# Upper and lower parts of stationary weights element by element in one tile, 128 bytes off a multiple of 256

## The chip, the cores and the metric

The kernel runs on one core of one Trainium2 chip. The metric is device time in microseconds of one execution. TensorE multiplies, ScalarE (ACT) and VectorE (DVE) move and convert tiles, GpSimd (POOL) helps with sums, SyncE (SP) issues the large DMAs.

## The reference

Two pre-norm residual layers over 512 tokens of width 1024, each a token mixer and a squared-ReLU MLP, all in float32:

```python
for i in range(DEPTH):                       # DEPTH = 2
    h = rmsnorm(x, norm_mix_g[i])
    if i % N_MIXERS == 0:
        h = chunked_spatial_gating(h, a_w_in, a_b_in, a_v_norm_g, a_w_s, a_b_s, a_w_out)
    else:
        h = retention(h, b_w_in, b_head_norm_g, b_w_out)
    x = x + h
    h = rmsnorm(x, norm_ffn_g[i])
    x = x + squared_relu_mlp(h, mlp_w1[i], mlp_w2[i])   # relu(h @ w1) ** 2 @ w2, width 4096
return rmsnorm(x, final_norm_g)
```

The gating mixer projects to two halves `u` and `v` of width 2048, mixes `v` over chunks of 128 tokens and multiplies. The retention mixer has four heads with queries and keys of 256, values of 512 and a gate `g`.

## The kernel before

Every large product is made of three matmuls on numbers of type fp32r, which TensorE reads at one pass. Both factors are split into an upper part (the value rounded to fp32r, names ending in H) and a lower part (what is left, names ending in L), and `mm3` adds upper by upper, upper by lower and lower by upper into one PSUM tile. In the profile these are lines 215, 216 and 217. In "out<-a,b" of a matmul, a is the moving operand (512 columns mostly) and b the stationary one (128 by 128, loaded by an LDWEIGHTS, shown as PEld, before its matmul).

The weights are 60 raw tiles of 1 MB, each brought by DMA into one of two buffers (`RAW_BUFS`) and cut into two pieces of 128 partitions by 1024 elements. There are three ways to cut:

- `pieces_f`: eight blocks of 128 by 128 along the contraction. The weights are stationary and the activations moving. It serves `up`, `dn` (the down projection of layer 0), `u`, `g`, `qk`.
- `pieces_o`: four blocks of 128 by 256, stationary too, for the mixers' output projections `o` and `ro`.
- `pieces_t`: two blocks of 128 by 512. The weights are moving, and slices of the activations are stationary. It serves `v`, `vv` and `dt` (the down projection of layer 1).

A piece takes 24 matmuls, with 8 to 16 more of another kind between pieces where attention, gating or transposes need them. The order of the work is written out by hand: `step` appends a function and its pieces to a list, and the last loop runs the list. In each step the function issues the matmuls, then `advance()` (the second halves of earlier evacuations), then `refill()`, then the evacuation of its own result.

`refill` prepares pieces ahead. `prep` takes the next piece of the order: it has the DMA of a coming raw tile issued on SP (`load_raws`), takes tiles (`prep_tiles`), has ScalarE round the raw piece into the upper part (the CAST of line 179), and has VectorE subtract that from the raw piece into the lower part (line 183). Upper parts are made three pieces ahead (`LOOK`) in four buffers, lower parts two ahead in three buffers. An engine works through its queue in order; semaphores hold it where a buffer is not free or an input is missing.

Where things lie: in each partition, `xT`, `hH`, `hL`, the raw tiles, the upper and lower weight tiles and the ten large buffers of the activations start on a multiple of 2048 bytes. The small constants do not: `onesr`, the all-ones stationary matrix of the norm's sums, starts at byte 17024, which is 128 more than a multiple of 256. Upper and lower weights are contiguous, 4096 bytes per partition each.

Of the kernel before, what the change touches and what calls it, by code (L numbers as in the profile page):

```python
# [11 lines left out]
F32R = mybir.dt.float32r  # L12
# [5 lines left out]
P = 128  # L18
# [14 lines left out]
class Raw:  # L33


    def __init__(self, src, parts=1):
        self.src, self.parts, self.tile, self.done = src, parts, None, 0


class Piece:  # L40


    def __init__(self, raw, view, shape):
        self.raw, self.view, self.shape = raw, view, shape
        self.hi = self.lo = None


def pieces_f(w, rows, cols):
# [9 lines left out]
def pieces_t(w, rows, cols, parts=1):  # L58

    out = []  # L60
    for r in range(rows[0], rows[1], 512):
        raw = Raw(w[r : r + 512, cols[0] : cols[1]].rearrange("(k p) n -> p k n", p=P), parts)
        for i in range(2):
            out.append(Piece(raw, (slice(None), slice(2 * i, 2 * i + 2), slice(None)), [P, 2, 512]))
    return out


# [11 lines left out]
def trunk(ctx, tc, x, norm_mix_g, norm_ffn_g, a_w_in, a_b_in, a_v_norm_g, a_w_s, a_b_s, a_w_out,  # L79
          b_w_in, b_head_norm_g, b_w_out, mlp_w1, mlp_w2, final_norm_g, trig, decay, out):  # L80
    nc = tc.nc
# [3 lines left out]
    wts = ctx.enter_context(tc.tile_pool(name="wts", bufs=3))  # L85
# [1 line left out]
    work = ctx.enter_context(tc.tile_pool(name="work", bufs=2))  # L87
    psum = ctx.enter_context(tc.tile_pool(name="psum", bufs=6, space=PSUM))

    RAW_BUFS, LOOK = 2, 3  # L90

    def big(shape, dt, name):
        return bigp.tile(shape, dt, tag="big", name=name)
# [16 lines left out]
    def f32(ap):  # L110
        return ap.bitcast(F32)
# [48 lines left out]
    def load_raws(upto):  # L160
        while pos["raw"] < min(upto, len(raws)):
            r = raws[pos["raw"]]
            while r.done < r.parts:
                load_part(r)
            pos["raw"] += 1

    def prep_tiles(i):
        p = order[i]
        p.hi = wts.tile(p.shape, F32R, tag="wH", name=f"wH{i}", bufs=4)
        p.lo = wts.tile(p.shape, F32R, tag="wL", name=f"wL{i}", bufs=3)  # L170

    def prep(upto, low=None):

        low = upto if low is None else low
        while pos["piece"] < min(upto, len(order)):
            p = order[pos["piece"]]
            load_raws(raws.index(p.raw) + RAW_BUFS)
            prep_tiles(pos["piece"])
            nc.scalar.copy(out=p.hi, in_=p.raw.tile[p.view])  # L179
            pos["piece"] += 1  # L180
        while pos["low"] < min(low, len(order)):
            p = order[pos["low"]]
            nc.vector.tensor_sub(out=p.lo, in0=p.raw.tile[p.view], in1=f32(p.hi))  # L183
            pos["low"] += 1

    def launch(g):
# [11 lines left out]

    def refill():
        n = pos["done"]  # L200
        prep(n + (LOOK if n >= 4 else 1), n + (LOOK - 1 if n >= 4 else 1))

    def step(fn, *ps):
        for p in ps:
# [107 lines left out]
    def feat(p, bufs, evac, name, behind=None):  # L312

        def run(p):
            ps = acc(name)
            mm_f(p, ps, *bufs(), range(8), 7)
            advance()
            refill()
            if behind:
                behind()  # L320
            launch(evac(ps))
        step(run, p)

    def feat_late(p, q, evacs, name):

        def run(p, q):
            pa, pb = acc(f"{name}a"), acc(f"{name}b")
            flush()
            for r, ps in ((p, pa), (q, pb)):
                mm_f(r, ps, hH, hL, range(7), 7)  # L330
            for r, ps in ((p, pa), (q, pb)):
                mm_f(r, ps, hH, hL, [7], 7)
            advance()
            refill()
            launch(evacs[0](pa))
            launch(evacs[1](pb))
        step(run, p, q)

    def tokens(plist, bufs, evac, name, behind=None, last=None):

        accs = {}
        behind = behind or {}

        def one(i):
            def run(p):
                if i == 0:
                    for n in range(NT):
                        accs[n] = acc(f"{name}_{n}")
                aH, aL = bufs()
                for n in range(NT):  # L350
                    s = slice(n * P, (n + 1) * P)
                    for k in range(2):
                        kk = 2 * i + k
                        mm3(accs[n], aH[kk][:, s], aL[kk][:, s], p.hi[:, k, :], p.lo[:, k, :], kk == 0, kk == 7)
                advance()
                refill()
                if i in behind:
                    behind[i]()
                if i == 3:
                    for n in range(NT):  # L360
                        launch(evac(n, accs[n]))
            return run

        for i, p in enumerate(plist[:2] if last else plist):
            step(one(i), p)
        if last:
            step(lambda *ps: last(bufs, accs, evac, *ps), *plist[2:])
# [161 lines left out]

    nrm = norm("mix0")  # L530
    vl = [pieces_t(win, (0, D), (GW + 512 * j, GW + 512 * (j + 1)), parts=4 if j == 0 else 1) for j in range(4)]
    accs0 = {}

    def two_chunks(i):

        prep(i + 2)
        for k in (2 * i + 2, 2 * i + 3):
            x_chunk(k)
        for k in (2 * i, 2 * i + 1):
            squares(k, MIX)  # L540

    def v0(i):
        def run(p):
            if i == 0:
                for n in range(NT):
                    accs0[n] = acc(f"v0_{n}")
            if i in (1, 2):
                two_chunks(i)
            for k in range(2):
                kk = 2 * i + k  # L550
                if i == 0 and k == 1:
                    two_chunks(0)
                if i == 3:
                    prep(5 + k)
                    if k == 0:
                        squares(6, MIX)
                        squares(7, MIX)
                    next(nrm)
                wh, wl = p.hi[:, k, :], p.lo[:, k, :]
                for j, (h, w) in enumerate(((hH, wh), (hH, wl), (hL, wh))):  # L560
                    for n in range(NT):
                        nc.tensor.matmul(accs0[n], lhsT=h[kk][:, n * P : (n + 1) * P], rhs=w, start=kk == 0 and j == 0, stop=kk == 7 and j == 2)
                if i == 2 and k == 0:
                    columns(rows, 16, 80)
            if i == 3:
                for n in range(NT):
                    launch(evac_v(0)(n, accs0[n]))
                next(nrm)
        return run
# [236 lines left out]
    def v_unit(h, behind=None):  # L806
        tokens(pieces_t(bw, (0, D), (VW + h * DV, VW + (h + 1) * DV)), hs, evac_vv(h), f"vv{h}", behind)
# [112 lines left out]
    def down_t(q):  # L920
        do(flush)
        for c in range(2):
            tokens(pieces_t(mlp_w2[1], (1024 * q, 1024 * (q + 1)), (512 * c, 512 * (c + 1))), acts(q), evac_last(q, c), f"dt{q}{c}",
                   last=ends if q == 3 and c == 1 else None)
# [32 lines left out]
    for _ in range(5):  # L957
        nc.tensor.matmul(warm[:, 0:P], lhsT=ident, rhs=ident, start=True, stop=True)
    columns(rows2, 0, 16)
    prep_tiles(0)  # L960
    for k in range(2):
        p = order[0]
# [56 lines left out]
```

## Time and profile before

| | |
|---|---|
| median of 3 runs | 1406.9 us (1406.83 to 1407.25) |
| profiled execution | 1407.72 us, span of its instructions 1406.0 us |
| TensorE busy with matmuls | 1390.5 us, 6290 matmuls |
| TensorE busy with weight loads | 1155.4 us, 6290 loads |
| VectorE / ScalarE / GpSimd busy | 793.0 / 507.2 / 127.7 us |
| casts of weights (ScalarE) | 239, mean 1045 ns |
| subtractions of weights (VectorE) | 239, mean 1282 ns |
| DMA | 135.23 MB, mean 96 GB/s |

The durations of matmuls overlap, since a matmul starts before the one ahead has drained. What a matmul costs is the distance between its start and the next one's. Weight loads run beside matmuls. The granted TensorE clock is 0.998 of full speed on average.

### The profile page before, as it was taken

How to read it: one execution, taken by the hardware profiler on the slowest of the kernel's cores; microseconds unless marked ns; L12 is line 12 of the kernel's file. 1: busy time of each engine (PE TensorE's matmuls, PEld its weight loads, DVE VectorE, ACT ScalarE, POOL GpSimd, SP SyncE). 2: the span in 40 equal slices, each digit the busy share in tenths (PEclk: the TensorE clock that was granted, in tenths of full speed). 3: DMA queues.
4: the chain of work that ended last, by engine and by line, in shares of the span. 5: the costliest groups of instructions: out<-in, count | busy, mean ns of one | idle time of the engine just before them, and what ended most of it. 6: DMA issues, size and time to landing. Idle time of an engine off the chain costs nothing.

```text
span 1406.0 us, 15372 instructions
## 1 busy us (share of the span) xinstructions
PE 1390.5 (99%) x6290; PEld 1155.4 (82%) x6290; DVE 793.0 (56%) x1102; ACT 507.2 (36%) x721; POOL 127.7 (9%) x98
## 2 busy tenths in 40 slices
PE   8999999999999999999999999999999999999997
PEld 7888888888888888888888888888888888888885
DVE  6757765775444445476647574564685443434335
ACT  4656633334413223123334323333334422313222
POOL 3010111220000000011111100110130000000002
PEclk9999999999999999999999999999999999999999
DMA  6332222232223322423222131132122332232221
GB/s 225 109 116 90 72 90 88 81 120 90 90 90 104 106 90 90 148 89 108 90 78 72 60 120 60 62 118 90 61 90 91 120 104 90 93 117 91 90 90 60
DMA packets 106101, 135.23 MB, mean 96 GB/s; under 512 B 2400, under 2 KB 79792, under 8 KB 105776
## 3 DMA queue, kind: packets, MB, share of 16 engines
q1 hardware_dynamic: 106000, 134.26, 29.4%
q8 instruction: 49, 0.80, 0.2%
q14 instruction: 20, 0.16, 0.0%
q10 hardware_dynamic: 32, 0.01, 0.0%
HBM read 132.16 MB, written 2.10 MB: 95 GB/s over the span
## 4 chain that ended last, share of the span: by engine, by line
PE 96%; DVE 3%; POOL 0%; ACT 0%; DMA 0%; issue 0%; SPq 0%; ACTq 0%; DVEq 0%
PE up L217 8%; PE up L216 8%; PE up L215 8%; PE dn L217 4%; PE dn L216 4%; PE dn L215 4%; PE dt L216 4%; PE dt L217 4%; PE dt L215 4%; PE g L215 2%; PE qk L215 2%; PE vv L216 2%; PE g L216 2%; PE vv L215 2%; PE g L217 2%; PE vv L217 2%
## 5 line engine op out<-in xcount | busy, mean ns | idle before, releaser
L183 DVE TENSOR_TENSOR wL<-raw,wH 128x1024 fp32r<-128x1024 f32 x239 | 305.9, 1282 | 112.8 <-PE dt L216 65.5
L179 ACT CAST wH<-raw 128x1024 fp32r<-128x1024 f32 x239 | 249.7, 1045 | 264.7 <-PE dt L217 114.9
L215 PE MATMUL up<-hH,wH 128*128 128x512 f32 x480 | 187.2, 390 | 0.0
L217 PE MATMUL up<-hH,wL 128*128 128x512 f32 x480 | 186.8, 389 | 0.0
L216 PE MATMUL up<-hL,wH 128*128 128x512 f32 x480 | 186.8, 389 | 0.0
L631 DVE TENSOR_TENSOR aH<-r 128x512 fp32r<-128x512 f32 x64 | 45.0, 703 | 159.5 <-ACT r L629 159.4
L216 PEld LDWEIGHTS up<-hL,wH 128*128 128x128 f32 x480 | 90.1, 188 | 18.7
L215 PEld LDWEIGHTS up<-hH,wH 128*128 128x128 f32 x480 | 90.1, 188 | 18.7
L217 PEld LDWEIGHTS up<-hH,wL 128*128 128x128 f32 x480 | 90.1, 188 | 18.7
L215 PE MATMUL dn<-aH,wH 128*128 128x512 f32 x256 | 99.6, 389 | 0.0
L216 PE MATMUL dn<-aL,wH 128*128 128x512 f32 x256 | 99.6, 389 | 0.0
L217 PE MATMUL dn<-aH,wL 128*128 128x512 f32 x256 | 99.6, 389 | 0.0
L215 PE MATMUL dt<-wH,aH 128*128 128x512 f32 x256 | 99.6, 389 | 0.0
L216 PE MATMUL dt<-wL,aH 128*128 128x512 f32 x256 | 99.6, 389 | 0.0
L217 PE MATMUL dt<-wH,aL 128*128 128x512 f32 x256 | 99.6, 389 | 0.0
L629 ACT ACTIVATE r<-up 128x512 f32<-128x512 f32 x60 | 35.9, 598 | 166.7 <-PE up L217 166.7
L239 POOL TENSOR_TENSOR ssq<-ssq,sq 128x512 f32<-128x512 f32 x28 | 43.0, 1537 | 401.6 <-ACT sq L238 401.3
L501 DVE TENSOR_TENSOR xs<-dn,wide 128x512 f32<-128x512 f32 x32 | 22.1, 692 | 74.5 <-PE dn L217 74.5
L215 PEld LDWEIGHTS dt<-wH,aH 128*128 128x128 f32 x256 | 48.0, 188 | 10.1
L216 PEld LDWEIGHTS dn<-aL,wH 128*128 128x128 f32 x256 | 48.0, 188 | 10.0
L215 PEld LDWEIGHTS dn<-aH,wH 128*128 128x128 f32 x256 | 48.0, 188 | 10.0
L216 PEld LDWEIGHTS dt<-wL,aH 128*128 128x128 f32 x256 | 48.0, 188 | 9.9
(271 smaller groups left out, 2709.5 us busy)
## 6 DMA issues: line engine op xcount, KB each, us to landing
raw<-in_mlp_w_dram SPq DMA_DIRECT2D x64, 1024.0 KB, 5.1
raw<-in_b_w_in_dram SPq DMA_DIRECT2D x24, 1024.0 KB, 5.0
raw<-in_a_w_in_dram SPq DMA_DIRECT2D x14, 1024.0 KB, 5.2
raw<-in_a_w_out_dram SPq DMA_DIRECT2D x8, 1024.0 KB, 4.9
raw<-in_b_w_out_dram SPq DMA_DIRECT2D x8, 1024.0 KB, 4.9
raw<-in_a_w_in_dram SPq DMA_DIRECT2D x8, 256.0 KB, 6.7
out_dram<-out SPq DMA_DIRECT2D x8, 256.0 KB, 2.1
xr<-in_x_dram SPq DMA_DIRECT2D x3, 512.0 KB, 6.6
```

What stands on the lines that cost most here:

```text
L179: nc.scalar.copy(out=p.hi, in_=p.raw.tile[p.view])
L183: nc.vector.tensor_sub(out=p.lo, in0=p.raw.tile[p.view], in1=f32(p.hi))
L215: nc.tensor.matmul(ps, lhsT=ah, rhs=bh, start=start, stop=False)
L216: nc.tensor.matmul(ps, lhsT=ah, rhs=bl, start=False, stop=False)
L217: nc.tensor.matmul(ps, lhsT=al, rhs=bh, start=False, stop=stop)
L239: nc.gpsimd.tensor_tensor(out=state["ssq"], in0=state["ssq"], in1=sq, op=ALU.add)
L501: nc.vector.tensor_mul(t, ps, r2bc)
L629: nc.scalar.activation(r, ps, AF.Relu)
L631: nc.vector.tensor_mul(h, r, r)
```

## The change

The upper and lower part of a piece now share one tile of 32 + 2048 + 32 elements, of which the middle 2048 are used. With 8448 bytes per tile, 33 times 256, the three tiles start on a multiple of 256 bytes and the used part 128 bytes behind it. In a stationary piece the parts alternate: element 0 of the upper, element 0 of the lower, element 1 of the upper, and so on, so each part has a step of 8 bytes. In a moving piece (`moving=True`) the upper part fills the first 1024 elements and the lower part the second, each contiguous. There are three such tiles, and both parts are made two pieces ahead. The large buffers behind them in memory move to 768 bytes past a multiple of 2048, still a multiple of 256.

```diff
 class Piece:
-    def __init__(self, raw, view, shape):
-        self.raw, self.view, self.shape = raw, view, shape
+    def __init__(self, raw, view, shape, moving=False):
+        self.raw, self.view, self.shape, self.moving = raw, view, shape, moving
         self.hi = self.lo = None
+
+    def src(self):
+        return self.raw.tile[self.view]
+
+    def place(self, t):
+        a = self.shape[1]
+        if self.moving:
+            self.hi, self.lo = (t[:, i * 1024 : (i + 1) * 1024].rearrange("p (a b) -> p a b", a=a) for i in range(2))
+        else:
+            v = t.rearrange("p (a b i) -> p a b i", a=a, i=2)
+            self.hi, self.lo = v[:, :, :, 0], v[:, :, :, 1]
...
-            out.append(Piece(raw, (slice(None), slice(2 * i, 2 * i + 2), slice(None)), [P, 2, 512]))
+            out.append(Piece(raw, (slice(None), slice(2 * i, 2 * i + 2), slice(None)), [P, 2, 512], moving=True))
...
-    RAW_BUFS, LOOK = 2, 3
+    RAW_BUFS, LOOK = 2, 2
...
     def prep_tiles(i):
         p = order[i]
-        p.hi = wts.tile(p.shape, F32R, tag="wH", name=f"wH{i}", bufs=4)
-        p.lo = wts.tile(p.shape, F32R, tag="wL", name=f"wL{i}", bufs=3)
+        p.place(wts.tile([P, 32 + 2048 + 32], F32R, tag="w", name=f"w{i}", bufs=3)[:, 32 : 32 + 2048])
...
-            nc.scalar.copy(out=p.hi, in_=p.raw.tile[p.view])
+            nc.scalar.copy(out=p.hi, in_=p.src())
...
-            nc.vector.tensor_sub(out=p.lo, in0=p.raw.tile[p.view], in1=f32(p.hi))
+            nc.vector.tensor_sub(out=p.lo, in0=p.src(), in1=f32(p.hi))
...
-        prep(n + (LOOK if n >= 4 else 1), n + (LOOK - 1 if n >= 4 else 1))
+        prep(n + (LOOK if n >= 4 else 1))
```

TensorE's and VectorE's instructions keep their order. On ScalarE each cast comes one piece later against the evacuations. These are ScalarE's rows in an up projection of layer 0, before; `r` and `rr` are evacuations of the PSUM tile named last, and the number behind `wH` is the piece's place in the order:

```order
L629 ACTIVATE r1_3813<-up03_1_3781 128x512
L630 ACTIVATE rr1_3814<-r1_3813 128x512
L179 CAST wH93_3844<-raw46_3736 128x1024
L629 ACTIVATE r2_3848<-up03_2_3818 128x512
L630 ACTIVATE rr2_3849<-r2_3848 128x512
L179 CAST wH94_3881<-raw47_3807 128x1024
```

The same place after the change:

```order
L641 ACTIVATE r1_3716<-up03_1_3687 128x512
L642 ACTIVATE rr1_3717<-r1_3716 128x512
L191 CAST w92_3749<-raw46_3675 128x1024
L641 ACTIVATE r2_3752<-up03_2_3721 128x512
L642 ACTIVATE rr2_3753<-r2_3752 128x512
L191 CAST w93_3783<-raw46_3675 128x1024
```

Between the evacuations of the second and third result stood the cast of piece 93; now it is that of piece 92. On VectorE the subtraction stood at piece 92 there already, before:

```order
L633 TENSOR_TENSOR aL3_0_3775<-rr1_3814,aH3_0_3774 128x512
L183 TENSOR_TENSOR wL92_3810<-raw46_3736,wH92_3809 128x1024
L631 TENSOR_TENSOR aH3_0_3774<-r2_3848 128x512
L633 TENSOR_TENSOR aL3_0_3775<-rr2_3849,aH3_0_3774 128x512
L183 TENSOR_TENSOR wL93_3845<-raw46_3736,wH93_3844 128x1024
```

And after:

```order
L645 TENSOR_TENSOR aL3_0_3681<-rr1_3717,aH3_0_3680 128x512
L195 TENSOR_TENSOR w92_3749<-raw46_3675,w92_3749 128x1024
L643 TENSOR_TENSOR aH3_0_3680<-r2_3752 128x512
L645 TENSOR_TENSOR aL3_0_3681<-rr2_3753,aH3_0_3680 128x512
L195 TENSOR_TENSOR w93_3783<-raw46_3675,w93_3783 128x1024
```

Nothing moved on VectorE, but the subtraction of piece 92 now reads a cast that was issued in the same `refill`, not in the one before.

## The prediction

> **What bounds the kernel now.** I read the page first, then the chain that ended last, then single matmuls in the timeline, because the first two leave nothing else to read. These are the span, the busy times and the chain's shares by engine:
>
> ```profile
> span 1406.0 us, 15372 instructions
> PE 1390.5 (99%) x6290; PEld 1155.4 (82%) x6290; DVE 793.0 (56%) x1102; ACT 507.2 (36%) x721; POOL 127.7 (9%) x98
> PE 96%; DVE 3%; POOL 0%; ACT 0%; DMA 0%; issue 0%; SPq 0%; ACTq 0%; DVEq 0%
> ```
>
> TensorE is the bound from one end to the other; no other engine's time counts unless it makes TensorE wait. So the question is only how far apart matmuls start. The timeline of a down projection answers it (columns: start, duration, engine and line; durations overlap, the starts are what counts):
>
> ```profile
> 600.16 0.39 PE L215 MATMUL dn<-aH,wH 128*128 128x512 f32 x1
> 600.17 0.19 PEld L216 LDWEIGHTS dn<-aL,wH 128*128 128x128 f32 x1
> 600.39 0.39 PE L216 MATMUL dn<-aL,wH 128*128 128x512 f32 x1
> 600.39 0.19 PEld L217 LDWEIGHTS dn<-aH,wL 128*128 128x128 f32 x1
> 600.62 0.39 PE L217 MATMUL dn<-aH,wL 128*128 128x512 f32 x1
> ...
> 605.60 0.39 PE L215 MATMUL dn<-aH,wH 128*128 128x512 f32 x1
> ```
>
> From 600.16 to 605.60 lie 24 matmuls (one piece): 5.44 us, 226.7 ns each. Each load of the next weights starts with the matmul before it and is over in 0.19 us, so a load does not hold up the next matmul by being late. Is 227 ns the array's own time? The first token-stage matmuls and later ones of the same shape say no:
>
> ```profile
> 9.55 1.91 PE L562 MATMUL v<-wL,hH 128*128 128x512 f32 x4
> 11.26 1.18 PE L562 MATMUL v<-wH,hL 128*128 128x512 f32 x4
> ...
> 20.40 1.07 PE L562 MATMUL v<-wL,hH 128*128 128x512 f32 x4
> 21.31 1.07 PE L562 MATMUL v<-wH,hL 128*128 128x512 f32 x4
> ```
>
> Four matmuls take 1.71 us at first (427 ns each) and 0.91 us later (227 ns). The ratio is 1.88. If the first stretch is the same work at half pace, the full pace would be 213.8 ns, and 13 ns of each matmul are something else. A second view says what. Around the two matmuls with `onesr` as weights, the starts spread:
>
> ```profile
> 312.82 0.39 PE L215 MATMUL up<-hH,wH 128*128 128x512 f32 x1
> 313.04 0.39 PE L216 MATMUL up<-hL,wH 128*128 128x512 f32 x1
> 313.27 0.40 PE L217 MATMUL up<-hH,wL 128*128 128x512 f32 x1
> 313.50 0.40 PE L271 MATMUL st_ffn<-st_ffn,onesr 128*128 128x512 f32 x1
> 313.74 0.40 PE L272 MATMUL st_ffn<-st_ffn,onesr 128*128 128x512 f32 x1
> 313.98 0.40 PE L215 MATMUL up<-hH,wH 128*128 128x512 f32 x1
> ...
> 314.69 0.39 PE L215 MATMUL up<-hH,wH 128*128 128x512 f32 x1
> 314.91 0.39 PE L216 MATMUL up<-hL,wH 128*128 128x512 f32 x1
> ```
>
> No engine is waited for here, all matmuls have 512 columns, yet the distances run 0.22, 0.23, 0.23, 0.24, 0.24 and later 0.22 us. Of the operands in this stretch `onesr` alone lies 128 bytes off a multiple of 256; all others, moving and stationary, lie on one. So the distance depends on how the reading of the next weights and the reading of the moving operand meet in memory. I take the 13 ns as the price of two readers crossing.
>
> [...]
>
> **The change part by part.**
>
> *Interleaved weights.* How fast do the two readers walk? Short matmuls show the load's pace:
>
> ```profile
> 725.61 0.22 PE L215 MATMUL av<-pH,vvH 128*128 128x128 f32 x1
> 725.67 0.28 PE L216 MATMUL av<-pL,vvH 128*128 128x128 f32 x1
> 725.78 0.27 PE L217 MATMUL av<-pH,vvL 128*128 128x128 f32 x1
> 725.89 0.44 PE L215 MATMUL qk<-hH,wH 128*128 128x512 f32 x1
> ```
>
> With 128 columns and its weights there, a matmul takes 0.06 us; when it must wait for new weights, 0.11 us. So 128 weights are read in about 110 ns: 512 bytes per partition, 4.7 bytes per ns, against 2048 bytes in 227 ns, 9.0 bytes per ns, on the moving side. Today the moving reader runs through memory twice as fast and passes the weights' reader again and again (modulo 256 bytes). With the upper and lower parts in turn, a step is 8 bytes, so the weights' reader covers 1024 bytes in 110 ns, 9.3 bytes per ns: the same pace. Starting 128 bytes apart modulo 256, the two then stay apart. If crossings cost the 13 ns, most of it goes.
>
> The price per matmul has to be bounded. Lower end: 213.8 ns, nothing left over. Upper end: 240 ns, the rows at 313.50 and 313.74. The fastest distance in the trace is 0.22 us (314.69). I take 217 ns, the middle of 213.8 and 220, since the layout is made of what those rows make differ. The counts, by tile:
>
> ```profile
> L215 PE MATMUL up<-hH,wH 128*128 128x512 f32 x480 | 187.2, 390 | 0.0
> L215 PE MATMUL dn<-aH,wH 128*128 128x512 f32 x256 | 99.6, 389 | 0.0
> L215 PE MATMUL u<-hH,wH 128*128 128x512 f32 x128 | 50.6, 395 | 0.0
> L215 PE MATMUL up00a<-hH,wH 128*128 128x512 f32 x8 | 3.1, 389 | 0.0
> L215 PE MATMUL dt<-wH,aH 128*128 128x512 f32 x256 | 99.6, 389 | 0.0
> L215 PE MATMUL vv<-wH,hH 128*128 128x512 f32 x128 | 49.9, 390 | 0.0
> L215 PE MATMUL v<-wH,hH 128*128 128x512 f32 x96 | 37.4, 390 | 0.0
> L562 PE MATMUL v<-wH,hH 128*128 128x512 f32 x32 | 10.0, 437 | 0.0
> ```
>
> Each row stands for one of three terms. Weights are stationary in `up` (480), `dn` (256), in `u`, `o`, `g`, `qk`, `ro` (128 each, one row for five) and in four groups of 8: 1408, times 3, is 4224 matmuls. 4224 x (226.7 - 217.0) ns = 41.0 us less.
>
> *Moving weights.* In `dt`, `vv` and `v` the weights are the moving operand: 256 + 128 + 96 + 32 = 512, times 3, is 1536 matmuls. Their halves stay contiguous but now start 128 off a multiple of 256, with the stationary activations still on one. Before, both were on one. Bounds: 213.8 ns below, 240 ns above. The nearest row is the matmul at 313.27, in which contiguous weights 128 bytes off were read beside an undisturbed stream: 0.23 us, which with the following 0.24 I read as about 6 ns more. So 1536 x 6 ns = 9.2 us more; the ends are -20 and +20 us.
>
> *Casts and subtractions in 8-byte steps.* ScalarE writes every second element, VectorE reads and writes so. What they take now, and VectorE's busiest stage (last row: stretch, its length, busy time and count for PE, PEld, DVE, ACT, POOL):
>
> ```profile
> L179 ACT CAST wH<-raw x239: 1030/1046/1074, 10.7 to 1376.2; 128x1024 fp32r<-128x1024 f32 x120
> L183 DVE TENSOR_TENSOR wL<-raw,wH x239: 1209/1219/2344, 11.7 to 1379.2; 128x1024 fp32r<-128x1024 f32 x120
> 160.00:330.00 170.00, 170.00 (x795) 142.19 (x795) 114.86 (x154) 68.58 (x96) 26.77 (x19) 1.00 0.29 93
> ```
>
> No row shows such steps. Bounds: unchanged, or doubled (2.09 and 2.44 us; the longest of the subtractions takes 2.34 now). I take unchanged, the rows of the same instructions. Doubled, the 170 us stage, with 31 pieces of 5.44 us, gets 31 x 1.22 = 38 us more on VectorE: 153 of 170 us, still under TensorE. [...]
>
> *Three buffers, lead of two pieces.* A cast waits for the buffer of the piece before the current one, as now. It runs in the current piece and is needed two pieces later: 2 x 5.44 = 10.9 us for a cast and a subtraction of 1.05 + 1.22 = 2.3 us; ScalarE is busy 68.58 us for 31 pieces in the stage above, 2.2 us a piece with the cast, so little stands ahead of it. Now the subtraction waits for a cast of the same refill; queued behind it on VectorE are the next piece's evacuations, which wait for TensorE anyway. Cost 0; the cover is one whole piece. Were it gone, TensorE would wait up to about 2 us a piece. The DMA of the next raw tile still starts when the last subtraction from its buffer ends, and is first needed one piece later than now. What waits TensorE has today stays at the start:
>
> ```profile
> PE xt L397 <- DMA xr<-in_x_dram: 1.8, 1, 1.8
> PE warm L958 <- POOL ident masks.py:199: 1.4, 1, 1.4
> ```
>
> Sum, against the profiled execution's 1407.7 us (span 1406.0 and 1.7 around it): 1407.7 - 41.0 + 9.2 = 1375.9. The median of the runs is 0.8 us lower, so 1375 us.
>
> **The rivals.**
> - *Slower: the cost goes by the memory that the weights' reader walks through.* It walks twice as far, so 13 ns become 26 and the distance is 240 ns, which the `onesr` rows show to be possible. 4224 x 13.3 = 56 us more, with the moving term 65: 1463 to 1472. It decides once distance, not crossing, sets the price. For it: a crossing at the pace of 9 bytes per ns that starts on the wrong foot would never end. Against it: the `onesr` load walks no farther than others and costs more.
> [...]
> - *Slower by the neighbours:* the moving term at its upper end (20 us) with half the gain on the stationary side (20 us) cancels to 1407; if ScalarE and VectorE double and stall the stages around 160 to 330 us by another tenth, 17 us, it ends at 1424.
>
> **How the numbers follow.** Chances: my forecast 0.63 (its own range 1357 to 1396: 213.8 ns and no moving cost, or 220 ns and 20 us); no change 0.11; twice the walk 0.17; neighbours 0.09. Within 0.2% (2.8 us, about what can be told from no change) lies the second case alone, so faster 0.63, same 0.11, slower 0.26. The range 1356 to 1440 leaves out most of the third case and a little below.
>
> **What the profile after would show.** A piece of `dn` or `up` in 24 x 217 ns = 5.2 us instead of 5.44; loads still 188 ns; `dt` and `vv` matmuls about 233 ns apart; TensorE busy near 1359 us; the cast near 1046 and the subtraction near 1219 ns; TensorE's waits as short as now. I am wrong if the stationary-weight matmuls keep 227 ns or go to 240, or if `dt` moves by more than `dn`.

## The result: 34.7 us slower, and the profile after

| | before | after |
|---|---|---|
| median of 4 runs each | 1407.08 us (1406.83 to 1408.5) | 1441.75 us (1440.93 to 1443.13) |
| ratio | 1 | 1.0245, 95% interval 1.0228 to 1.0263 |

The forecast was 1375 us; the kernel got slower, and ended 1.75 us above the top of the range. These are the span, busy times and the chain's shares by engine of the kernel after:

```profile
span 1441.4 us, 15423 instructions
PE 1422.5 (99%) x6290; PEld 1188.7 (82%) x6290; DVE 796.7 (55%) x1102; ACT 520.7 (36%) x721; POOL 125.9 (9%) x98
PE 89%; DVE 5%; ACT 3%; issue 1%; POOL 0%; DMA 0%; SPq 0%; ACTq 0%; DVEq 0%
```

TensorE is still the bound, with the same 6290 matmuls, and its busy time rose from 1390.5 to 1422.5 us. So the question is again how far apart matmuls start. The tables by stretch give it without rounding. Each row below runs from the first to the last start of 192 matmuls, which is 191 distances, in one unit of eight pieces (for `dt` two units of four). Columns: stretch and length, busy time and count of PE, PEld, DVE, ACT, POOL, granted clock, DMA share, GB/s. Before, for `up`, `dn` and `dt`:

```profile
336.32:379.62 43.30, 43.30 (x193) 35.85 (x191) 20.16 (x24) 17.38 (x24) 0.00 (x0) 1.00 0.29 96
597.44:640.74 43.30, 43.30 (x193) 35.85 (x191) 35.40 (x38) 12.07 (x15) 9.65 (x6) 1.00 0.27 88
1308.44:1351.73 43.29, 43.29 (x192) 35.85 (x191) 16.27 (x17) 9.57 (x10) 0.00 (x0) 1.00 0.34 115
```

After, the same three, and as a fourth row a stretch from the stage of `u` and `o`:

```profile
350.02:394.23 44.21, 44.21 (x193) 37.38 (x192) 20.89 (x24) 18.03 (x24) 0.00 (x0) 1.00 0.30 95
616.63:660.83 44.20, 44.20 (x192) 37.37 (x191) 32.96 (x38) 12.59 (x15) 9.66 (x6) 1.00 0.26 85
1341.06:1385.63 44.57, 44.57 (x193) 35.85 (x191) 16.09 (x17) 9.51 (x10) 0.00 (x0) 1.00 0.31 103
160.00:345.00 185.00, 181.85 (x827) 152.67 (x826) 124.50 (x164) 77.14 (x105) 29.04 (x21) 1.00 0.28 92
```

Length by 191: 226.7 ns before in all three; after 231.4 ns for `up` and `dn` (turned stationary weights, 217 forecast) and 233.4 ns for `dt` (moving weights, 233 forecast). PE's column equals the length in every such unit, so no engine is waited for there: the matmuls themselves are farther apart. The busy time of 191 loads rose from 35.85 to 37.37 us, 188 to 196 ns a load. In the fourth row TensorE is idle for 3.15 us; the row of before for 160 to 330 us had none. The timeline of a `dn` piece shows 24 matmuls in 5.55 us, 5.44 before:

```profile
616.63 0.39 PE L227 MATMUL dn<-aH,w 128*128 128x512 f32 x1
616.86 0.39 PE L228 MATMUL dn<-aL,w 128*128 128x512 f32 x1
617.09 0.39 PE L229 MATMUL dn<-aH,w 128*128 128x512 f32 x1
617.32 0.39 PE L227 MATMUL dn<-aH,w 128*128 128x512 f32 x1
617.55 0.40 PE L228 MATMUL dn<-aL,w 128*128 128x512 f32 x1
617.79 0.40 PE L229 MATMUL dn<-aH,w 128*128 128x512 f32 x1
...
622.18 0.39 PE L227 MATMUL dn<-aH,w 128*128 128x512 f32 x1
```

Mostly 0.23 us, sometimes 0.24: the distance does not hold still but runs through a short repeating series. The cast and the subtraction, with minimum, median and maximum in ns:

```profile
L191 ACT CAST w<-raw x239: 1030/1117/1167, 10.9 to 1414.1; 128x1024 fp32r<-128x1024 f32 x120
L195 DVE TENSOR_TENSOR w<-raw,w x239: 1211/1226/2184, 12.0 to 1415.1; 128x1024 fp32r<-128x1024 f32 x120
```

The 8-byte step costs ScalarE 72 ns a cast: the median is 1117 ns here, and 1045 with the same tiles and contiguous parts (three_buffers below). It costs VectorE nothing that shows: 1226 ns here and 1225 in three_buffers.

### The profile page after: what moved, and what is told of

Its sections match the earlier page's. It is cut to its first block, busy times and chain, and to the rows that moved or that the text cites. A ratio compares the mean times of both kernels' runs of the same rounds, so it can differ in the third digit from the quotient of the medians.

```text
span 1441.4 us, 15423 instructions
## 1 busy us (share of the span) xinstructions
PE 1422.5 (99%) x6290; PEld 1188.7 (82%) x6290; DVE 796.7 (55%) x1102; ACT 520.7 (36%) x721; POOL 125.9 (9%) x98
## 4 chain that ended last, share of the span: by engine, by line
PE 89%; DVE 5%; ACT 3%; issue 1%; POOL 0%; DMA 0%; SPq 0%; ACTq 0%; DVEq 0%
PE up L227 8%; PE up L228 8%; PE up L229 8%; PE dn L227 4%; PE dn L228 4%; PE dn L229 4%; PE dt L227 4%; PE dt L229 4%; PE dt L228 4%; PE g L227 2%; PE qk L227 2%; PE vv L227 2%; PE vv L229 2%; PE vv L228 2%; PE g L228 2%; PE qk L228 2%
## 5 line engine op out<-in xcount | busy, mean ns | idle before, releaser
L195 DVE TENSOR_TENSOR w<-raw,w 128x1024 fp32r<-128x1024 f32 x239 | 299.4, 1253 | 204.9 <-ACT w L191 203.5
L191 ACT CAST w<-raw 128x1024 fp32r<-128x1024 f32 x239 | 263.3, 1103 | 264.1 <-PE dt L229 120.6
L227 PE MATMUL up<-hH,w 128*128 128x512 f32 x480 | 189.3, 394 | 0.0
L228 PE MATMUL up<-hL,w 128*128 128x512 f32 x480 | 188.8, 393 | 0.0
L229 PE MATMUL up<-hH,w 128*128 128x512 f32 x480 | 188.8, 393 | 0.0
L229 PEld LDWEIGHTS up<-hH,w 128*128 128x128 f32 x480 | 93.9, 196 | 17.2
L227 PEld LDWEIGHTS up<-hH,w 128*128 128x128 f32 x480 | 93.9, 196 | 17.1
L229 PE MATMUL dt<-w,aL 128*128 128x512 f32 x256 | 101.1, 395 | 0.0
L228 PE MATMUL dt<-w,aH 128*128 128x512 f32 x256 | 101.1, 395 | 0.0
L227 PE MATMUL dt<-w,aH 128*128 128x512 f32 x256 | 101.1, 395 | 0.0
L227 PE MATMUL dn<-aH,w 128*128 128x512 f32 x256 | 100.7, 393 | 0.0
L228 PE MATMUL dn<-aL,w 128*128 128x512 f32 x256 | 100.7, 393 | 0.0
L229 PE MATMUL dn<-aH,w 128*128 128x512 f32 x256 | 100.7, 393 | 0.0
L227 PEld LDWEIGHTS dn<-aH,w 128*128 128x128 f32 x256 | 50.1, 196 | 9.2
L229 PEld LDWEIGHTS dn<-aH,w 128*128 128x128 f32 x256 | 50.1, 196 | 9.2
```

The lines of the kernel that those rows point to most:

```text
L191: nc.scalar.copy(out=p.hi, in_=p.src())
L195: nc.vector.tensor_sub(out=p.lo, in0=p.src(), in1=f32(p.hi))
L227: nc.tensor.matmul(ps, lhsT=ah, rhs=bh, start=start, stop=False)
L228: nc.tensor.matmul(ps, lhsT=ah, rhs=bl, start=False, stop=False)
L229: nc.tensor.matmul(ps, lhsT=al, rhs=bh, start=False, stop=stop)
```

## The experiments

Two theories stood at first. The walk theory: the time goes by what the load of weights does (how far it reads, how fast, how much). The distance theory: it goes by how far apart the addresses of the two readers are, modulo some length, and turning is not what matters. The third suspect was the lead of two pieces, to which the prediction gave 0.

### The change taken apart

All four have the tile of three buffers; edits are against the kernel after. **three_buffers**: parts contiguous again, on a multiple of 256.

```diff
-        if self.moving:
+        if True:
...
-        p.place(wts.tile([P, 32 + 2048 + 32], ...)[:, 32 : 32 + 2048])
+        p.place(wts.tile([P, 32 + 2048 + 32], ...)[:, 0:2048])
```

> Only the shared tile with three buffers and the lead of two pieces is kept; both parts are contiguous and start on a multiple of 256 bytes, as before. If the loss lies in how the two readers meet in memory (both theories, offset and turn), matmuls are 226.7 ns apart again and the time is 1407 us, within 3. If the shorter lead costs, single waits of TensorE for cast or subtraction remain and it is 1410 to 1415.

**offset_only**: contiguous, but 128 bytes off.

```diff
-        if self.moving:
+        if True:
```

> Contiguous parts, but 128 bytes off. Theory offset: what slows is two readers that lie 128 bytes apart modulo 256, so up and dn matmuls stay near 231 ns and dt near 233; 1438 to 1445 us. Theory turn: the 8-byte step slows the stationary side, the offset only the moving one; up and dn return to 226.7 ns, dt stays at 233: 1407 + 1536 x 6.4 ns = 1417 us.

**turn_only**: stationary parts in turn, everything on a multiple of 256.

```diff
-        p.place(wts.tile([P, 32 + 2048 + 32], ...)[:, 32 : 32 + 2048])
+        p.place(wts.tile([P, 32 + 2048 + 32], ...)[:, 0:2048])
```

> Parts in turn for stationary weights, but on a multiple of 256 bytes; moving weights on one too. Theory offset: 226.7 ns or less everywhere, 1407 us or below. Theory turn: up and dn stay near 231.4 ns, dt returns to 226.7: 1407 + 4224 x 4.7 ns = 1427 us. The theory of the prediction (equal pace, apart by 128) expects the two readers on top of each other, 240 ns: 1463 us.

**moving_back**: as after, but moving pieces start on a multiple of 256.

```diff
-        p.place(wts.tile([P, 32 + 2048 + 32], ...)[:, 32 : 32 + 2048])
+        o = 0 if p.moving else 32
+        p.place(wts.tile([P, 32 + 2048 + 32], ...)[:, o : o + 2048])
```

> As after the change, but moving weights start on a multiple of 256 bytes. Offset and turn both: dt, vv and v return to 226.7 ns, up and dn stay at 231.4: 1442 - 1536 x 6.4 ns = 1432 us. If dt and vv do not return, the cause on the moving side is another one (the activations' buffers lie 768 bytes past a multiple of 2048 now): 1442 us.

| | us, median of 4 | ratio to before (1407.25) | `dn` ns | `dt` ns |
|---|---|---|---|---|
| three_buffers | 1415.17 | 1.0058 (1.0041 to 1.0075) | 226.7 | 226.7 |
| offset_only | 1443.73 | 1.0261 (1.0245 to 1.0276) | 232.4 | 232.4 |
| turn_only | 1440.03 | 1.0233 (1.0218 to 1.0248) | 233.4 | 226.7 |
| moving_back | 1433.2 | 1.0187 (1.0172 to 1.0202) | 231.4 | 226.7 |

The distances come from rows by stretch, length over 191: `dn` of three_buffers, `dn` and `dt` of offset_only, `dn` and `dt` of turn_only, `dt` of moving_back:

```profile
589.63:632.93 43.30, 43.30 (x193) 35.85 (x192) 27.21 (x33) 9.46 (x11) 4.89 (x3) 1.00 0.30 98
```

```profile
615.98:660.37 44.39, 44.39 (x193) 35.99 (x191) 33.33 (x38) 12.05 (x15) 9.68 (x6) 1.00 0.26 85
1342.12:1386.51 44.39, 44.39 (x193) 35.99 (x191) 16.09 (x17) 9.51 (x10) 0.00 (x0) 1.00 0.31 104
```

```profile
616.68:661.25 44.57, 44.57 (x193) 36.86 (x191) 32.93 (x38) 12.56 (x15) 9.63 (x6) 1.00 0.26 84
1340.49:1383.78 43.29, 43.29 (x192) 35.85 (x191) 16.09 (x17) 9.53 (x10) 0.00 (x0) 1.00 0.32 105
```

```profile
1332.87:1376.17 43.30, 43.30 (x192) 35.85 (x191) 16.09 (x17) 9.53 (x10) 0.00 (x0) 1.00 0.31 105
```

The runs make a ladder: before to three_buffers +7.9 us, on to moving_back (turned and 128 off, stationary only) +18.0, on to after (moving weights 128 off) +8.6. These steps add up to the whole by construction; what tests them is the count of matmuls. By the units above, 4224 x 4.7 ns = 19.9 us stand against 18.0, and 1536 x 6.7 = 10.3 against 8.6. Both are too much because `dn` and `dt` stand for the rest there. Over all starts of the traces from 30 us on (steps above 262 ns left out as waits), stationary weights go from a mean of 227.0 ns in three_buffers to 231.5 in moving_back, and moving weights from 227.0 in moving_back to 233.0 in after. That makes 4224 x 4.5 = 19.0 and 1536 x 6.0 = 9.2 us. What is left over is within the spread of the runs: moving_back alone ran from 1432.5 to 1434.77 us.

Each of the two halves of the layout does harm alone: 128 bytes off without turning is as slow as after, turning without the offset nearly so. The 1440.03 us of turn_only fit none of the expectations (1407, 1427 or 1463 us). The turn theory comes nearest once the 7.9 us of the lead are added, which all four runs share. In turn_only the upper parts start at a difference of 0 and every distance in `dn` is 233 or 234 ns, so turning matters too, and the distance theory as first put is not the whole. The large buffers, which moved by 768 bytes in all four runs, are not a cause: `dt` is at 226.7 ns in three of them.

### The lead

**lead_two** is the kernel before, with the upper part made two pieces ahead instead of three, and nothing else.

```diff
-        prep(n + (LOOK if n >= 4 else 1), n + (LOOK - 1 if n >= 4 else 1))
+        prep(n + (LOOK - 1 if n >= 4 else 1))
```

> The kernel before with its seven separate tiles and layouts; only the casts are made two pieces ahead instead of three. If the 8 us of the run with three buffers come from the shorter lead (the subtraction waits for a cast of the same refill behind ScalarE's tanh), it is again 1415 us, with the waits at the start of o and u pieces. If they come from sharing one tile between both parts, 1407 us.

1414.53 us (1413.66 to 1414.77) beside 1407.08, ratio 1.0052 (1.0036 to 1.0069): 7.4 of the 7.9 us of three_buffers are the lead. Where it waits, by stretch, and how, in the timeline:

```profile
160.00:330.00 170.00, 166.74 (x772) 137.35 (x771) 117.39 (x157) 69.74 (x98) 28.14 (x21) 1.00 0.29 93
```

```profile
168.19 0.68 DVE L425 SCALAR_TENSOR_TENSOR us<-us,uz 128x512 f32<-128x512 f32 x1
...
168.90 0.63 ACT L426 ACTIVATE us<-us 128x512 f32<-128x512 f32 x1 [0.70 <-DVE us L425]
...
169.44 1.04 ACT L179 CAST wH<-raw 128x1024 fp32r<-128x1024 f32 x1
...
170.51 1.23 DVE L183 TENSOR_TENSOR wL<-raw,wH 128x1024 fp32r<-128x1024 f32 x1 [1.64 <-ACT wH L179]
...
171.79 0.19 PEld L217 LDWEIGHTS o<-yH,wL 128*128 128x128 f32 x1 [0.56 <-DVE wL L183]
```

Of 170 us TensorE is idle for 3.3, and has started 772 matmuls where it had started 795: 23 x 0.227 = 5.2 us behind. The chain reads upward: the load waits 0.56 us for the lower part, the subtraction stood 1.64 us for its cast, and the cast was queued on ScalarE behind an activation that itself waited 0.70 us for VectorE. With the cast a piece earlier, the subtraction hardly met this; the waits say so, before, in lead_two and after the change (engine and line that waits, what ends it; total us, times, longest):

```profile
DVE wL L183 <- ACT wH L179: 5.1, 3, 2.8
```

```profile
DVE wL L183 <- ACT wH L179: 70.2, 68, 5.8
```

```profile
DVE w L195 <- ACT w L191: 203.5, 160, 5.8
```

Most of this waiting is VectorE's alone: of the 203.5 us after the change, 5.9 us reach TensorE as waits for lower parts.

### Is it the weights' walk?

The rest starts from three_buffers, where `up`, `dn` and `dt` stand at 226.7 ns; what is given is what each does to single units. These are single executions without an interval, and they are read by the distances, not by the total. **still_readers**: in `up` all 128 stationary columns read one element of the piece, so the load walks nowhere; in `dn` all 512 moving columns read one. Those products are not the reference's.

```diff
+            if still == "up":
+                h, l = (w[:, 0:1].broadcast_to([P, P]) for w in (h, l))
...
+            if still == "dn":
+                m = [w[:, 0:1].broadcast_to([P, T]) for w in m]
```

> Three buffers, contiguous. In up the 128 stationary columns all read one element, in dn the 512 moving columns read one element (both change the result); all else is as before. If the 13 ns come from the weights' reader walking through memory beside the moving one, up falls from 226.7 to 214 to 218 ns; if from the moving side, dn does. If it is a fixed handover of weights, both stay at 226.7.

The total was 1412.0 us. The rows of `up` and `dn`:

```profile
342.64:386.89 44.25, 44.25 (x192) 36.07 (x191) 20.88 (x24) 17.33 (x24) 0.00 (x0) 1.00 0.30 95
600.40:641.62 41.22, 41.22 (x192) 36.10 (x191) 32.99 (x38) 12.00 (x15) 9.53 (x6) 1.00 0.28 95
```

With the load standing still, 231.7 ns, more than 226.7. With the moving side still, 215.8, beside ordinary loads. The walk theory expects a gain in the first and none in the second. 215.8 is also the lowest distance that any run showed for 512 columns, 10.9 ns under 226.7.

**narrow_loads**: in six of eight blocks, `up` loads 32 of the 128 stationary columns and `dn` 64. The rest of those products is left out.

```diff
+            c = {"up": 32, "dn": 64}.get(name, P) if 0 < k < 7 else P
+            mm3(ps[0:c], p.hi[:, k, 0:c], p.lo[:, k, 0:c], bH[k], bL[k], k == 0, k == last)
```

> Contiguous, on a multiple of 256, three buffers. For six of eight contraction blocks only 32 stationary columns are loaded in up and 64 in dn (this leaves out part of the result). If the cost arises while weights are read beside the moving operand, those matmuls go from 226.7 ns towards 215.8, with 32 columns (a quarter of the 11 ns) near 218.5, with 64 near 221. If the moving reader alone pays it, or a handover of fixed size, they stay at 226.7.

The total was 1422.46 us. The rows of `up` and `dn`:

```profile
343.81:387.86 44.05, 44.05 (x193) 24.53 (x192) 20.89 (x24) 17.39 (x24) 0.00 (x0) 1.00 0.29 94
608.61:652.39 43.78, 43.78 (x193) 28.21 (x191) 33.30 (x38) 12.07 (x15) 9.69 (x6) 1.00 0.26 87
```

The loads are a third and a fifth shorter in sum (24.53 and 28.21 us, 35.85 for full ones), yet the distances are 230.6 and 229.2 ns. Reading fewer weights buys nothing. With both runs the walk theory has fallen.

### Is it the distance of the addresses?

**both_128** is offset_only with the moving activations `hH`, `hL` 128 bytes off as well: now the two readers of `up` are both 128 off.

```diff
-    hH = [keep.tile([P, T], F32R, name=f"hH{k}") for k in range(KD)]
+    hH = [keep.tile([P, T + 64], F32R, name=f"hH{k}")[:, 32 : 32 + T] for k in range(KD)]
... (hL alike)
```

> As the run with the offset alone, but the moving activations hH and hL also start 128 bytes off a multiple of 256. Theory that only the distance between the two readers modulo 256 counts: up, u, g and qk return from 232.4 to 226.7 ns, dn and ro (moving tiles still on a multiple) stay at 232.4. Theory that a stationary operand off a multiple of 256 is itself slow: all stay at 232.4.

The total was 1426.93 us. The rows of `up`, `dn`, `dt`:

```profile
344.05:387.35 43.30, 43.30 (x193) 35.87 (x191) 20.88 (x24) 17.35 (x24) 0.00 (x0) 1.00 0.30 96
609.02:653.59 44.57, 44.57 (x193) 35.88 (x191) 33.31 (x38) 12.06 (x15) 9.70 (x6) 1.00 0.26 84
1325.24:1369.64 44.40, 44.40 (x193) 36.05 (x191) 16.08 (x17) 9.51 (x10) 0.00 (x0) 1.00 0.30 103
```

`up` is back at 226.7 ns; `dn` and `dt`, whose other operand still lies on a multiple of 256, stay at 233.4 and 232.5. So for contiguous weights what counts is the difference of the two addresses, not where each lies. A difference of 128 bytes has no single value: `dn` is at 233.4 here and at 232.4 in offset_only, and `dt` at 232.4 in offset_only and at 233.4 after the change. Which of the two it is no run explains, so a difference of 1 ns between offsets below means nothing.

The sweeps give each unit of `up`, `dn` and `dt` its own offset. **sweep_turn** has turned stationary weights, **sweep_flat** contiguous ones.

```diff
+TURN, UP, DN, DT = True, [16, 32, 48, 64, 80, 96, 160, 192], [8, 112, 224, 240], [16, 32, 64, 80, 96, 160, 192, 224]
...
+        t = t[:, self.off : self.off + 2048]
-        if self.moving:
+        if not self.turn:
...
+            p.off, p.turn = UP[4 * l + q] // 4, TURN
```

In sweep_flat `TURN` is False and the last list is `[8, 48, 112, 144, 176, 208, 240, 256]`.

> Three buffers; one execution with a layout of its own in each part of the two MLPs, read part by part. Parts in turn, start in bytes off a multiple of 256: up of layer 0: 16, 32, 48, 64; up of layer 1: 80, 96, 160, 192; dn: 8, 112, 224, 240. Moving dt, contiguous: 16, 32, 64, 80, 96, 160, 192, 224. Theory of a meeting modulo 256: the distance depends on the offset, with at least one below 226.7 ns, perhaps near 217. Theory of a lock: 0 and contiguous is the best case, nothing goes below 226.7 ns, all others lie between 227 and 234.

> As the sweep of parts in turn, but contiguous parts: up 16, 32, 48, 64, 80, 96, 160, 192; dn 8, 112, 224, 240; dt 8, 48, 112, 144, 176, 208, 240, 256 bytes. Both theories have 256 at 226.7 ns if the period is 256. Meeting: some offset below 226.7. Lock: none below, and small offsets already near 232.

Their totals were 1431.78 and 1429.42 us. Mean distance in ns by offset in bytes (0 and 128 from turn_only, after, three_buffers and offset_only; a few waits in the units of 16, 80 and 96 are left out):

| offset | stationary, turned | stationary, contiguous | moving weights |
|---|---|---|---|
| 0 | 233.4 | 226.7 | 226.7 |
| 8 | 231.7 | 230.7 | 232.5 |
| 16 | 233.3 | 226.8 | 231.6 |
| 32 | 232.2 | 233.3 | 233.4 |
| 48 | 231.1 | 233.3 | 233.2 |
| 64 | 230.0 | 233.3 | 229.0 |
| 80 | 231.9 | 232.0 | 231.1 |
| 96 | 233.3 | 234.3 | 233.3 |
| 112 | 230.0 | 233.3 | 231.1 |
| 128 | 231.4 | 232.4 | 232.4 |
| 144 | | | 233.2 |
| 160 | 233.3 | 233.3 | 234.2 |
| 176 | | | 231.0 |
| 192 | 233.3 | 228.9 | 233.3 |
| 208 | | | 234.6 |
| 224 | 233.3 | 233.3 | 233.3 |
| 240 | 231.4 | 228.4 | 236.2 |
| 256 | | | 226.7 |

Three of the rows, `up` at 64 turned, and of sweep_flat `dt` at 240 and at 256 (these two with 95 distances):

```profile
522.31:566.24 43.93, 43.93 (x193) 37.10 (x192) 20.80 (x24) 16.94 (x22) 0.00 (x0) 1.00 0.27 89
```

```profile
1372.37:1394.81 22.44, 22.44 (x96) 18.07 (x95) 7.13 (x8) 5.57 (x8) 1.29 (x1) 1.00 0.20 70
1395.05:1416.59 21.54, 21.54 (x97) 17.84 (x95) 10.85 (x30) 5.80 (x12) 6.40 (x5) 1.00 0.07 25
```

21.54 us over 95 is 226.7 ns: at 256 the distance is what it is at 0, at 240 it is 236.2. So the value of 0 comes back at 256 bytes, which was tried in `dt` alone; of the smaller offsets only 16 comes as near to 226.7, and that for contiguous stationary weights alone. Turned weights never fall below 230.0 ns at any offset tried, so no start gives them the gain that the prediction expected. Contiguous ones never fall below 226.7. Before's layout, contiguous and with difference 0, stands at the best value found for whole operands, and the smaller offsets follow no slope.

### Is the cost on the moving side, and once per matmul?

**short_walks**: in `up` the 512 moving columns are the first w columns over and over, w from 256 to 2, so those products are not the reference's. **orders**: the 512 columns are read and written in another order, h stretches in turn, b columns of each at a time.

```diff
+WALK = {"up00": 256, "up01": 128, "up02": 64, "up03": 32, "up10": 16, "up11": 8, "up12": 4, "up13": 2}
...
+            if walk:
+                m = [v[:, 0:walk].unsqueeze(1).broadcast_to([P, T // walk, walk]) for v in m]
```

> Three buffers, contiguous, on a multiple of 256. In up the moving operand reads its first w columns again and again until 512 are done (this changes the result): w = 256, 128, 64, 32 in layer 0, 16, 8, 4, 2 in layer 1. One element again and again took 215.8 ns. If each change of a 16-byte group costs, 4 and 2 are near 216 and 8 and more near 227. If the distance between the two readers modulo 256 is what counts, 64 columns (256 bytes) and more are near 227 and the change comes at 32 or below. Handover theory: all 226.7.

```diff
+WAYS = {"up00": (2, 4), "up01": (2, 8), "up02": (2, 16), "up03": (2, 32), "up10": (2, 64), "up11": (2, 128), "up12": (4, 4), "up13": (8, 4),
+        "dn00": (4, 16), "dn01": (4, 32), "dn02": (2, 2), "dn03": (16, 4)}
...
+            if way:
+                m = [v.rearrange("p (h n b) -> p n h b", h=way[0], b=way[1]) for v in m]
```

> Three buffers, contiguous, on a multiple of 256. In up and dn the 512 moving columns are read (and written to PSUM) in another order: h stretches in turn, b columns at a time. up of layer 0: h x b = 2x4, 2x8, 2x16, 2x32; up of layer 1: 2x64, 2x128, 4x4, 8x4; dn: 4x16, 4x32, 2x2, 16x4. If the 11 ns above 215.8 are the moving reader coming back to the same part of memory too soon, some order brings it nearer 216 ns. If any walk over 2048 bytes costs it, all stay between 226 and 234; 2x2 breaks 16-byte groups and may be slower still.

Totals 1412.73 and 1470.11 us. short_walks: 226.7 ns for 256, 128 and 64 columns, 236.7 for 32, 242.0 for 16, and 215.8 for 8, 4 and 2. The rows for 64, 32 and 4:

```profile
430.08:473.37 43.29, 43.29 (x193) 35.85 (x191) 20.80 (x24) 16.26 (x22) 0.00 (x0) 1.00 0.28 91
517.12:562.32 45.20, 45.20 (x193) 35.97 (x191) 20.80 (x24) 16.26 (x22) 0.00 (x0) 1.00 0.27 88
1186.63:1227.85 41.22, 41.22 (x192) 36.10 (x191) 20.24 (x23) 16.18 (x22) 0.00 (x0) 1.00 0.28 92
```

The cost is gone only where the moving operand never leaves 32 bytes (8 columns); 64 or 128 bytes gone over again are worse than a plain walk. In orders, two stretches in turn give 226.7 ns with 128 columns at a time, 236.7 with 32, 240.0 with 16, 243.4 with 8, about 250 with 4 and 333 with 2. The rows for 8, 32 and 2:

```profile
346.31:392.79 46.48, 46.48 (x193) 36.20 (x192) 20.87 (x24) 17.34 (x24) 0.00 (x0) 1.00 0.28 90
528.31:573.51 45.20, 45.20 (x193) 36.12 (x192) 20.78 (x24) 16.25 (x22) 0.00 (x0) 1.00 0.27 86
573.74:637.41 63.67, 63.67 (x192) 37.24 (x191) 20.23 (x24) 9.50 (x10) 0.00 (x0) 1.00 0.30 105
```

Four stretches give 233.4 ns with 32 columns at a time, 231.2 with 16 and 268.0 with 4; eight and sixteen stretches of 4 give 278.1 and 246.8. No other order than the plain one is faster. Reading 32 columns over and over and reading two stretches 32 at a time take the same 45.20 us, although one writes PSUM in order and the other does not, which suggests that at that size the reading alone sets the distance. In the other units of orders the reading and the writing change together, and no run tells them apart.

**fewer_columns**: 22 of 24 matmuls of a unit stream fewer than 512 columns, and the rest of those products is left out. If the cost is paid per column, it shrinks with them; if once per matmul, it stays.

```diff
+COLS = {"up00": 504, "up01": 496, "up02": 480, "up03": 448, "up10": 416, "up11": 384, "up12": 352, "up13": 320, "dn00": 508, "dn01": 488, "dn02": 472, "dn03": 256}
...
+                n = T if (k, i) in ((0, 0), (7, 2)) else cols
+                nc.tensor.matmul(ps[:, 0:n], lhsT=w[:, k, :], rhs=m[k][:, 0:n], ...)
```

> Three buffers, contiguous, on a multiple of 256. In up and dn 22 of a piece's 24 matmuls stream fewer columns (this leaves out part of the result): up of layer 0: 504, 496, 480, 448; of layer 1: 416, 384, 352, 320; dn: 508, 488, 472, 256. [...]

The total was 1355.41 us. The rows for 496, 448, 352 and 320 columns:

```profile
344.31:386.52 42.21, 42.21 (x193) 35.85 (x191) 20.89 (x24) 17.36 (x24) 0.00 (x0) 1.00 0.30 98
515.65:554.82 39.17, 39.17 (x192) 35.88 (x191) 20.79 (x24) 16.24 (x22) 0.00 (x0) 1.00 0.30 99
1150.60:1182.46 31.86, 31.86 (x192) 31.16 (x191) 20.26 (x23) 16.22 (x22) 0.00 (x0) 1.00 0.36 119
1226.26:1255.51 29.25, 29.25 (x193) 28.59 (x191) 20.05 (x23) 16.25 (x22) 0.00 (x0) 1.00 0.39 128
```

Of 191 distances 15 are of 512 columns; by the starts of the matmuls these take 233 ns in the unit of 352 and 232 in that of 320. That leaves (31.86 - 3.50) / 176 = 161.1 ns and (29.25 - 3.48) / 176 = 146.4 ns. In proportion to the columns 226.7 ns would become 155.8 and 141.7. A straight line through 512 and 320 columns has 0.418 ns per column and 12.7 ns per matmul; it gives 159.8 ns at 352 and 119.7 at 256, where 119.5 was measured (waits left out). So most of the cost is paid once per matmul.

It is not of one fixed size, though. The other units lie above that line: 384 columns by 0.9 ns (174.1), 416 by 1.7, 448 by 2.9 (202.9), 472 by 3.0, 480 by 3.4, 488 by 8.7 (225.4), 496 by 0.4 (220.4), 504 by 3.9, 508 by 2.7. With 508 columns a matmul even takes longer than with 512, 227.7 ns. Multiples of 64 columns (256 bytes) do not stand apart: 448 is one and lies 2.9 ns above, 496 is none and lies 0.4.

What settles there, and what does not: the cost needs a moving operand that leaves 32 bytes (215.8 ns at 8 columns, 242.0 at 16), it falls mostly once per matmul (12.7 ns by the line), and its size goes by the difference of the two addresses within 256 bytes (226.7 ns at 0, 232.4 at 128, contiguous) and by the step of the weights (at 0, 226.7 ns contiguous and 233.4 turned). It does not shrink with fewer weights (230.6 ns with 32 columns). Why a matmul costs just that, why its size changes with the number of columns, and why a load that stands still or is narrow raises it by 2.5 to 5 ns, stays open. No version with the whole product beats the kernel before.

## Why the prediction was wrong, step by step

- **What bounds the kernel**: right. TensorE is busy for 99% before and after, and the pace of matmuls decided 27 of the 35 us.
- **Interleaved weights, -41.0 us: the step that failed.** Measured +18.0 us; 231.4 ns where 217.0 was forecast. Two observations under it held: 11 to 13 ns of each 226.7 are not owed to the number of columns alone (215.8 was reached, and the line over columns leaves 12.7; the 213.8 of the prediction rested on its assumption that the first stretch ran at half pace, which no run tested), and the distance depends on how the two operands lie (226.7 against 232.4 ns). What failed is the sentence that made them a mechanism, "I take the 13 ns as the price of two readers crossing", with the pace that followed from it. No row showed a reader at another pace. What the runs showed in its place: turned weights, which the prediction gave the same pace as the moving side, stand at 230.0 to 233.4 ns at every start tried; taking the load's walk away altogether raised the distance to 231.7; and offset_only, with the old pace and the new offset, is as slow as the whole change. The price goes by the difference of the addresses and the step, and for whole operands the distance is lowest at 226.7 ns, where the kernel stood before. The rows around `onesr` had shown a stationary operand 128 bytes off beside a moving one on a multiple of 256, at 233 to 241 ns. The prediction took them for its upper bound and let an argument without a row set the term. Why the readers interfere as they do stays open.
- **Moving weights, +9.2 us**: right in sign and size, +8.6 us, 233.4 ns for 233 forecast. It was the term priced from the nearest row without a story. The row had the stationary operand off and the term has the moving one, and both_128 shows why this may be carried over. That 6 ns came so close is in part luck: the rows gave 0.23 and 0.24 us, and other offsets between 8 and 240 bytes run from 229.0 to 236.2.
- **Casts and subtractions, 0**: right in effect. Casts rose by 7% and subtractions not at all against three_buffers; and three_buffers, without 8-byte steps, already has the waiting, 3.29 us of TensorE's idle time from 160 to 345 us beside 3.15 after.
- **Three buffers and the lead, 0: wrong by 7.9 us.** "The cover is one whole piece" was counted as busy time, 2.2 us of 5.44. But ScalarE's queue stands still behind activations that wait for VectorE (0.70 us in the rows of lead_two), and VectorE's behind the cast (1.64 us there); in the stage of `u` and `o` the two waits add up past the cover, and 0.56 us reach TensorE. The prediction looked at ScalarE's queue by its busy share, and left out the time in which that queue stands still.
- **The rivals.** "Slower by the walk" had the sign and not the mechanism: twice the walk would have been 240 ns and 1463 us; it was 231.4, and a load without a walk is no cheaper. "No change" fell: the rows of `dt` of moving_back and of after, between which those units differ by 128 bytes alone, have 226.7 and 233.4 ns. "Neighbours" put the moving term and the stalls on the right side, but held on to half the gain.
- **The marks set down ahead.** Of the two that were to refute it, "keep 227 or go to 240" did not occur, since 231.4 lies between; "`dt` moves by more than `dn`" did (6.7 against 4.7 ns). Loads went to 196 ns, not 188; TensorE's busy time to 1422.5, not 1359.
- **The forecast's own range** does not come out of its terms: 213.8 ns with no moving cost is 54 us less, about 1353 us and not 1357, and 220 ns with 20 us is about 1399 and not 1396. This did not decide anything.

## What to carry to other kernels

Where matmuls follow each other without a wait, look at the distance of their starts to a tenth of a nanosecond over some 200 of them, keep the weights contiguous, and keep the moving and the stationary operand a multiple of 256 bytes apart: here turned weights stand at 230.0 to 233.4 ns, and a difference of 128 bytes alone costs 5.7 to 6.7 ns on 227. A mechanism inferred from a few rows is a hypothesis; run the part of the change that tests it alone (here the offset without the turning) before adding up 4224 of its gain. When a lead is shortened, count the cover on each engine by what stands in its queue, waits included, and not by its busy share.

## What was not expected of the hardware

- The distance of matmuls of 512 columns ran from 215.8 to 333 ns with the same array work, by addresses alone: 226.7 plain, 215.8 within 32 bytes, 242.0 within 64 bytes, 333 in steps of 8 bytes between two stretches (there PSUM is written in that order too).
- Where the distance holds still from matmul to matmul, it took the values 226.7 (before), 233.3 (turn_only) and 240.0 ns (orders, 16 columns at a time), which lie 6.7 ns apart, the time of 16 columns at 0.418 ns. In other layouts it runs through a series, in `dn` after the change 228 to 236 ns with a period of seven matmuls.
- Less work at the load made matmuls slower: 230.6 ns with 32 weight columns, 231.7 with one element for all, beside 226.7 for whole loads.
- A load in 8-byte steps takes 196 ns, or 193 (36.86 us over 191) on a multiple of 256, for 188 contiguous. This is shorter than the distance of matmuls in all these units, so its length alone does not set the pace.
